# A hybrid encoder block: gate and up projections of ten pairs as token-major quads, activations turned by VectorE and moved within SBUF

## The chip, the cores and the metric

The kernel runs on one core of a Trainium2 chip. The metric is the device time of one execution in microseconds; the time before is the median of three runs. A profile is one execution recorded by the hardware profiler. Its engines are TensorE (PE, with its weight loads as PEld), VectorE (DVE), ScalarE (ACT), GpSimd (POOL) and SyncE (SP), which issues DMA transfers; ACT and POOL issue some too.

## The reference

One layer of an encoder block on 512 tokens of width 1024, in float32: a combined input projection feeds a short convolution and a bidirectional retention, the two are gated and merged, and a feed-forward part follows. The change is in the feed-forward part:

```
h2 = rmsnorm(x, g_ffn)
x  = x + (silu(h2 @ w_ff_gate) * (h2 @ w_ff_up)) @ w_ff_down     # 1024 -> 2816 -> 1024
y  = rmsnorm(x, g_final)
```

## The kernel before

**Precision and Strassen.** Every matrix operand is split into a high and a low part (`split`, L200: ACT rounds to the high part at L203, VectorE subtracts to get the low part at L204), and each product is three matmuls: high by high, high by low, low by high. On top of that the large products use a Strassen scheme in Winograd's form: seven products of half-size operands in place of eight. The operand forms are called a11, a12, a22, s1 to s4 for activations and b11, b21, t1 to t4, b22 for weights. Weight forms t1 to t4 are sums of two weight quarters; VectorE adds them (L301) right before the split, except for a few weights listed in `SUMMED`, whose sums are made ahead of time in DRAM by accumulating transfers and only loaded.

**Two ways to lay out a product.** Feature-major (`prod`, L375, matmuls at L383): weights are the stationary operand, activations are the moving one, 256 columns per matmul, the result has features on the partitions and tokens along the free dimension. Token-major (`prod_tm`, L409, matmuls at L427): activations are stationary, weights are the moving operand, 512 columns per matmul, the result has tokens on the partitions. The mixers' projections, the output projections and the down product are token-major already.

**The feed-forward part before.** The 2816 inner features are 22 blocks of 128, or 11 pairs. A pair (`pair`, L1173) is one Strassen product whose two weight columns are 256 gate features and the same 256 up features; its seven products are feature-major, 24 narrow matmuls each. The results come out with features on the partitions, which is what the down product needs for its stationary operand, so `gated` (L1125) can build the activation forms at once: silu on ACT, a multiplication by the up half on VectorE (L1139), differences (L1155) and splits into high and low tiles. The first products of up to three pairs are run ahead (`FIRST_PRODUCTS`, `beside`). The pairs are worked in three parts of 3, 4 and 4 (`FF_PARTS`), each followed by its down product (`strassen` through `down`, L1223), in which two pairs' worth of rows are one unit of 512 columns by two. The first part's result is put in DRAM (`put_first`), added to the residual `ydr` later (`add_first`, behind a small POOL instruction called mark), the second part's is accumulated into `ydr` directly (`add_y`); the last part's joins the residual in SBUF (`snap_y`, `to_y`), is normalized and written out (`put`).

**What sets the order.** `plan` lists all weight units in the order of use. `take` (L321) hands out the next unit and splits ahead until `AHEAD` = 2 units are ready; `load_raws` keeps the raw loads on SP `LEAD` = 4 units ahead of that. The tile framework schedules instructions at compile time; each engine then works its own queue in order, with semaphore waits. `tc.issue_after` orders an engine's instructions behind a given one. Pools are small: 14 large tiles (`big`), of which the gate/up input's forms hold seven and one part's activation forms seven, 9 tiles of 512 columns (`tmp`), 8 PSUM banks, 2 tiles in `misc`.

## Time and profile before

| | before |
|---|---|
| median of three runs | 1023.7 us |
| lowest of them | 1023.23 us |
| span of the profiled execution | 1021.7 us |
| the runs' median less that span | 2.0 us |
| TensorE busy | 1013.2 us, 5586 matmuls |
| VectorE busy | 902.5 us |
| ScalarE busy | 548.4 us |
| GpSimd busy | 151.7 us |
| mean granted TensorE clock | 0.999 |
| read from HBM, written | 162.82 MB, 57.41 MB |

The profiled execution's own time is not given apart from its span; the last instruction ends 1021.7 us after the first, and the runs' median is 2.0 us above that. Busy time counts an engine's instructions, not its waits. Matmuls are pipelined, so their price is read from the distance of starts or from a stretch of the chain divided by its count, not from the duration of one. "Idle before" in a group of instructions is the time the engine stood still ahead of them, with what ended it. The feed-forward part runs from about 689 us to the end.

### The profile page before, as it was taken

The numbers are of one execution on the slowest core, as the hardware profiler recorded it, in microseconds if no ns is written. First come the engines' busy times: TensorE is split into PE (matmuls) and PEld (weight loads), VectorE is DVE, ScalarE is ACT, GpSimd is POOL, SyncE is SP. The second block draws the span as 40 slices with busy tenths as digits, with TensorE's granted clock in tenths as the row PEclk, the third lists the DMA queues.
The fourth block names the chain that finished last, engine by engine and source line by source line (L and its number), as shares of the span: only waits on it lengthen the run. The fifth ranks groups of instructions, "written<-read, shape, count | busy, mean of one in ns | idle before, by whom it ended". The sixth has DMA issues, their size and how long they took to land.

```text
span 1021.7 us, 14821 instructions
## 1 busy us (share of the span) xinstructions
PE 1013.2 (99%) x5586; PEld 883.2 (86%) x5586; DVE 902.5 (88%) x1161; ACT 548.4 (54%) x744; POOL 151.7 (15%) x238
## 2 busy tenths in 40 slices
PE   9999999999999999999999999999999999999997
PEld 7888888888888998888888888889998999899986
DVE  7878998979798888797989997999898999889996
ACT  7547665553655455343543325586654565556554
POOL 0030221222122003202122100020001410110011
PEclk9999999999999999999999999999999999999999
DMA  9525587695767657839597855484316562663523
GB/s 354 188 81 185 173 296 212 214 310 162 249 196 238 250 203 268 333 130 349 124 331 294 272 200 169 157 264 132 107 42 242 172 154 83 198 153 104 165 69 98
DMA packets 53992, 202.34 MB, mean 198 GB/s; under 512 B 7392, under 2 KB 7520, under 8 KB 49312
## 3 DMA queue, kind: packets, MB, share of 16 engines
q1 hardware_dynamic: 37600, 137.39, 39.0%
q0 software_dynamic: 16032, 63.71, 21.3%
q8 instruction: 44, 0.72, 0.3%
q10 hardware_dynamic: 288, 0.29, 0.1%
q14 instruction: 28, 0.23, 0.1%
HBM read 162.82 MB, written 57.41 MB: 216 GB/s over the span
## 4 chain that ended last, share of the span: by engine, by line
PE 98%; DVE 1%; ACT 0%; issue 0%; POOL 0%; POOLq 0%; ACTq 0%
PE bank L427 39%; PE bank L383 27%; PE bank L342 10%; PE bank L343 10%; PE bank L344 10%; PE bank L477 0%; PE bank L1053 0%; PE bank L998 0%; PE bank L662 0%; DVE raw L301 0%; DVE big L1296 0%; ACT whi L203 0%; DVE wlo L204 0%; POOL fin L1286 0%; POOL ac L1035 0%
## 5 line engine op out<-in xcount | busy, mean ns | idle before, releaser
L203 ACT CAST whi<-raw 128x1024 fp32r<-128x1024 f32 (+2 forms) x299 | 302.8, 1028 | 265.0 <-PE bank L427 67.1
L204 DVE TENSOR_TENSOR wlo<-raw,whi 128x1024 fp32r<-128x1024 f32 (+2 forms) x300 | 352.7, 1192 | 68.0 <-ACT whi L203 67.7
L383 PE MATMUL bank<-xform,whi 128*128 128x256 f32 x1424 | 258.2, 284 | 0.3 <-ACT whi L203 0.3
L383 PEld LDWEIGHTS bank<-xform,whi 128*128 128x128 f32 x1424 | 222.3, 192 | 2.0 <-ACT t L434 0.8
L383 PE MATMUL bank<-xform,wlo 128*128 128x256 f32 x712 | 200.7, 283 | 0.0
L427 PE MATMUL bank<-whi,big 128*128 128x512 f32 x596 | 187.0, 389 | 0.0
L427 PE MATMUL bank<-whi,xform 128*128 128x512 f32 x496 | 157.1, 390 | 0.0
L301 DVE TENSOR_TENSOR raw<-raw 128x1024 f32<-128x1024 f32 (+1 forms) x128 | 152.0, 1203 | 4.2 <-DMA raw<-wquad 3.3
L383 PEld LDWEIGHTS bank<-xform,wlo 128*128 128x128 f32 x712 | 136.4, 192 | 0.0
L427 PEld LDWEIGHTS bank<-whi,big 128*128 128x128 f32 x596 | 111.9, 188 | 23.8 <-ACT t L434 0.4
L427 PE MATMUL bank<-wlo,big 128*128 128x512 f32 x298 | 115.7, 389 | 0.0
L427 PEld LDWEIGHTS bank<-whi,xform 128*128 128x128 f32 x496 | 93.0, 188 | 19.7 <-DVE xform L204 0.6
L427 PE MATMUL bank<-wlo,xform 128*128 128x512 f32 x248 | 96.5, 389 | 0.0
L434 ACT COPY t<-bank 128x512 f32<-128x512 f32 x105 | 61.0, 587 | 56.3 <-PE bank L383 30.1
L342 PE MATMUL bank<-big,whi 128*128 128x512 f32 x220 | 85.7, 390 | 0.0
L344 PE MATMUL bank<-big,wlo 128*128 128x512 f32 x220 | 85.6, 389 | 0.0
L343 PE MATMUL bank<-big,whi 128*128 128x512 f32 x220 | 85.6, 389 | 0.0
L427 PEld LDWEIGHTS bank<-wlo,big 128*128 128x128 f32 x298 | 56.0, 188 | 11.4
L427 PEld LDWEIGHTS bank<-wlo,xform 128*128 128x128 f32 x248 | 46.6, 188 | 9.6
L342 PE MATMUL bank<-whi,big 128*128 128x512 f32 x128 | 49.8, 389 | 0.0
L343 PE MATMUL bank<-wlo,big 128*128 128x512 f32 x128 | 49.8, 389 | 0.0
L344 PE MATMUL bank<-whi,big 128*128 128x512 f32 x128 | 49.8, 389 | 0.0
(203 smaller groups left out, 1385.8 us busy)
## 6 DMA issues: line engine op xcount, KB each, us to landing
raw<-wquad SPq DMA_DIRECT2D x140, 512.0 KB, 4.7
raw<-wpack SPq DMA_DIRECT2D x42, 512.0 KB, 6.3
t_f<-wquad POOLq DMA_DIRECT2D x12, 512.0 KB, 8.0
z<-t POOLq DMA_DIRECT2D x24, 256.0 KB, 4.5
t_o<-wquad POOLq DMA_DIRECT2D x12, 512.0 KB, 6.7
zform<-z POOLq DMA_DIRECT2D x6, 1024.0 KB, 7.8
v<-t POOLq DMA_DIRECT2D x16, 256.0 KB, 5.7
sg<-t POOLq DMA_DIRECT2D x16, 256.0 KB, 4.8
```

The source lines that it names most:

```text
L203: first = (round or nc.scalar.copy)(hi, src)
L204: low_of[0] = nc.vector.tensor_tensor(out=lo, in0=src, in1=hi.bitcast(F32), op=ALU.subtract)
L301: nc.vector.tensor_tensor(out=t, in0=t, in1=raws[quad, more, u][:, 0:n], op=ALU.add)
L342: nc.tensor.matmul(ps, lh, rh, start=first, stop=False)
L343: nc.tensor.matmul(ps, lh, rl, start=False, stop=False)
L344: nc.tensor.matmul(ps, ll, rh, start=False, stop=last)
L383: nc.tensor.matmul(o, l[:, c], r[:, k], start=start and s == 0 and k == 0 and i == 0, stop=stop and k == 3 and i == 2, skip_group_check=True)
L427: nc.tensor.matmul(pss[tt], l, r[:, c], start=start and k == 0 and i == 0, stop=stop and k == n - 1 and i == 2, skip_group_check=True)
L434: nc.scalar.copy(t, ps)
```

## The change

Ten of the eleven pairs are joined two by two into five quads, the eleventh (`LONE`) stays a feature-major pair. A quad is a token-major Strassen product with 512 gate columns and 512 up columns: `first_a`, `first_b` and `rest` run the seven products through `prod_tm`, in two weight units of four blocks' rows each. `SUMMED` names one quad instead of two pairs, which is the same amount of weights. The parts are now 4, 4 and 3 pairs.

A quad's results have tokens on the partitions. `gated` forms silu times up on a 128x512 tile as before, and then VectorE transposes its 32x32 blocks into two tiles called turned (two transposes of 128x256 per tile, eight per quad). That leaves 32-row blocks at the wrong partitions; `scatter` moves them with 16 SBUF-to-SBUF transfers of 32 rows by 512 columns (64 KB), issued by POOL, into the space where the low parts of two forms will lie. `forms_of`, called after the fifth product of the following quad (in the lone pair after its fourth), builds the activation forms from there: one split of 1024 columns, one of 512, four differences and four splits of 512; it is ordered behind the last weight split issued.

The transposes leave tokens in an order in which each block of 128 holds four runs of 32 rows. So the rows of the residual and of the output are addressed by `rows` as 4 runs of 32 rows for each block: the accumulating writes to `ydr`, the loads of it at the end and the writes of the output all use it.

The order of the work: products of quads 0 and 1, quad 2, the down product of quads 0 and 1, quads 3 and 4, the down product of quads 2 and 3, the lone pair, the last down product of quad 4 and the lone pair.

```diff
-FF_PARTS = ((0, 3), (3, 4), (7, 4))
+FF_PARTS = ((0, 4), (4, 4), (8, 3))
+LONE = NFB // 2 - 1
...
-SUMMED = (("f", 0), ("f", 1), ("o",))
+SUMMED = (("g", 0), ("o",))
...
+    f(0, "b11", "b21")
+    f(1, "b11")
+    f(0, "t2", "t1", "t3", "t4", "b22")
+    f(1, "t1", "t2", "b21", "t3", "t4", "b22")
+    f(2, *FORMS)
+    d(*FF_PARTS[0])
+    f(3, *FORMS)
+    f(4, *FORMS)
+    d(*FF_PARTS[1])
+    f(LONE, *FORMS)
+    d(*FF_PARTS[2])
...
+    def act_forms_of(q, n, x1, x2):
+
+        tiles, i = slot(q)
+        hi, lo = ({k: area(t[j], i, n, k) for k, t in tiles.items()} for j in range(2))
+        split(flat(x1), flat(hi["a"]), flat(lo["a"]))
+        split(pairs(x2, 1), pairs(hi["z"], 0), pairs(lo["z"], 0))
+        x = [pairs(t, e) for t in (x1, x2) for e in range(2)]
+        s1, s3, s2, s4 = (t512()[:, 0:256 * n].rearrange("p (b t) -> p b t", t=P) for _ in range(4))
+        for o, a, b, op in ((s1, x[2], x[3], ALU.subtract), (s3, x[0], x[2], ALU.subtract),
+                            (s2, s1, x[0], ALU.subtract), (s4, x[1], s2, ALU.add)):
+            nc.vector.tensor_tensor(out=o, in0=a, in1=b, op=op)
+        for k, e, t in (("v", 1, s1), ("v", 0, s3), ("w", 0, s2), ("w", 1, s4)):
+            split(t, pairs(hi[k], e), pairs(lo[k], e))
...
+    def gated(i, j, g, u):
+
         s = t512()
         gate_of[0] = s
         nc.scalar.activation(s, g, AF.Silu)
         nc.vector.tensor_tensor(out=s, in0=u, in1=s, op=ALU.mult)
...
+        if i not in turned:
+            turned[i] = [misctile(D, "turned").rearrange("p (q i j r) -> p q i j r", q=2, i=4, j=4) for _ in range(2)]
+        for h, t in enumerate(turned[i]):
+            nc.vector.transpose(t[:, :, :, j, :].rearrange("p q i r -> p i q r"),
+                                s.rearrange("p (i q c) -> p i q c", i=4, q=4)[:, :, 2 * h:2 * h + 2, :])
+
+    def scatter(i):
+
+        tiles, at = slot(2 * i)
+        x = [area(tiles[k][1], at, 2, k).bitcast(F32) for k in "wv"]
+        for b in range(NB):
+            o = x[b // 2][:, b % 2].rearrange("p q e t -> p (q e t)")
+            for q in range(4):
+                nc.gpsimd.dma_start(o[32 * q:32 * q + 32],
+                                    turned[i][q // 2][32 * b:32 * b + 32, q % 2].rearrange("c i j r -> c (i j r)"))
+        scattered[i] = x
+
+    def forms_of(i):
+        with tc.issue_after(hi_of[0].ins), tc.issue_after(low_of[0].ins):
+            act_forms_of(2 * i, 2, *scattered[i])
...
+    def first_a(i, *between):
+
+        a = [bank(), bank()]
+        for u, hook in zip((0, 2), between or (None, None)):
+            prod_tm(4, of(XF[0, 0]), a, True, part=(u,))
+            if hook:
+                hook()
+        heads_of[i] = a, [snap(x) for x in a]
...
+    def rest(i, last_first=False, middle=True, behind=None):
+
+        a, p1 = heads_of[i]
+        d = [bank(), bank()]
+        if not last_first:
+            prod_tm(4, of(XF["s1"]), d, True)
+        prod_tm(4, of(XF["s2"]), a, False)
+        u2 = [snap(x) for x in a]
...
+        prod_tm(4, of(XF["s3"]), a, False)
+        u3 = [snap(x) for x in a]
+        for tt in range(2):
+            nc.vector.tensor_tensor(out=u3[tt], in0=d[tt], in1=u3[tt], op=ALU.subtract)
         if behind:
+            behind()
+        prod_tm(4, of(XF[1, 1]), a, False, True)
+        for tt in range(2):
+            gated(i, 2 + tt, a[tt], u3[tt])
+        prod_tm(4, of(XF["s4"]), d, False, True)
+        for tt in range(2):
+            nc.vector.tensor_tensor(out=u2[tt], in0=d[tt], in1=u2[tt], op=ALU.subtract)
+            gated(i, tt, p1[tt], u2[tt])
...
+    yrows = ydr.rearrange("(j b r) d -> b j r d", j=4, b=4)
+
+    def rows(nb, half, of=yrows):
+        return of[nb][:, :, half * 512:(half + 1) * 512]
 
     def add_y(t, nb, half):
-        nc.gpsimd.dma_start(out=ydr[nb * P:(nb + 1) * P, half * 512:(half + 1) * 512], in_=t, accum_op=ALU.add)
+        nc.gpsimd.dma_start(out=rows(nb, half), in_=t, accum_op=ALU.add)
...
+    rest(0, last_first=True, middle=False)
+    scatter(0)
+    rest(1, behind=lambda: forms_of(0))
+    scatter(1)
+    quad(2, lambda: forms_of(1))
+    down(4, put_first)
+    scatter(2)
+    quad(3, lambda: forms_of(2))
+    mark = small.tile([P, 1], F32, tag="mark", name="mark", bufs=1)
+    add_first(nc.gpsimd.tensor_scalar_add(mark, gate_of[0][:, 0:1], 0.0))
+    scatter(3)
+    quad(4, lambda: forms_of(3))
+    down(4, add_y)
+    scatter(4)
+    lone(lambda: forms_of(4))
...
     for half in (1, 0):
-        nc.sync.dma_start(y[half][:, 2:4, :], ydr[2 * P:, half * 512:(half + 1) * 512].rearrange("(n p) c -> p n c", p=P))
+        for nb in (2, 3):
+            nc.sync.dma_start(y[half][:, nb, :], rows(nb, half))
...
         for t, j, q in ((last, half, nc.sync), (other, 1 - half, nc.scalar if nb == 1 else nc.sync)):
-            q.dma_start(out[nb * P:(nb + 1) * P, j * 512:(j + 1) * 512], t)
+            q.dma_start(rows(nb, j, outrows), t)
...
+    outrows = out.rearrange("(j b r) d -> b j r d", j=4, b=4)
...
+        elif kind == "g":
+            w = (gate, up)[c].reshape(2, 4, P, -1)[r, u:u + n // 512, :, q[0] * 512:q[0] * 512 + 512]
```

More of the change, by code (lines that the diff above doesn't have):

```diff
@@ L115, in f, with d @@
         for n in names:
[L116 to L129 removed]
+            if q == LONE:
+                out.append(("q", ("f", q), n, 0, 4))
+            else:
+                for u in (0, 2):
+                    out.append(("q", ("g", q), n, u, 2))
+    def d(q0, n):
         units = [(name, u) for name in FORMS for u in range(0, n, 2)]
@@ L209, in split @@
                 op0=ALU.mult, op1=ALU.subtract)
+        hi_of[0] = first
         return first
@@ L1113, in block_kernel @@
     act = {}
[L1114 to L1135 removed]
+    slots = {}
@@ new lines, in lone_gated @@
+    def lone_gated(th, g, u):
+        s = t512()
+        nc.scalar.activation(s, g, AF.Silu)
+        if not lone_x:
+            lone_x.extend(t512().rearrange("p (b q e t) -> p b q e t", b=2, q=1, e=2) for _ in range(2))
+        for b, o in enumerate(lone_x):
+            for e in range(2):
+                x, y = (t.rearrange("p (e j b r) -> p e b j r", e=2, j=2, b=4)[:, e, 2 * b:2 * b + 2] for t in (u, s))
+                z = o[:, :, 0, e, 64 * th:64 * th + 64].rearrange("p b (j r) -> p b j r", j=2)
+                nc.vector.tensor_tensor(out=z, in0=x, in1=y, op=ALU.mult)
@@ L1136, in gated, with lone, ev11 @@
+    lone_x = []
+    def lone(behind):
+        got = {}
+        def ev11(t):
+            got.update(g=t)
+            behind()
+        forms = {"a11": XF[0, 0], "a12": XF[1, 0], "a22": XF[1, 1], **{n: XF[n] for n in ("s1", "s2", "s3", "s4")}}
+        fm_quad(forms, ev11, lambda ps: lone_gated(1, ps, got["u"]),
+                lambda t: got.update(u=t), lambda t: lone_gated(0, got["g"], t))
+        act_forms_of(LONE, 1, *lone_x)
+    turned = {}
+    def gated(i, j, g, u):
         s = t512()
@@ L1139, in gated @@
         nc.vector.tensor_tensor(out=s, in0=u, in1=s, op=ALU.mult)
-        def both(j, t):
-            split(t.rearrange("p (s t) -> p s t", s=2), *(x[:, :, i, :] for x in gates[q0][j]))
-        E, O = slice(0, 256), slice(256, 512)
-        if th == 1:
-            split(s[:, O], *(x[:, i, :] for x in act["a22"]))
-        else:
-            both(0, s)
-        gates[q, th] = s
-        if (q, 1 - th) not in gates:
-            return
-        x1, x2 = gates.pop((q, 0)), gates.pop((q, 1))
-        v, w = t512(), t512()
```

149 lines of the change are left out of this document (48 added, 101 removed).

## The prediction

> **What bounds the kernel now.** I read the page first: how much of the span each engine works, and which engine the chain of waits runs through.
>
> ```profile
> span 1021.7 us, 14821 instructions
> PE 1013.2 (99%) x5586; PEld 883.2 (86%) x5586; DVE 902.5 (88%) x1161; ACT 548.4 (54%) x744; POOL 151.7 (15%) x238
> PE 98%; DVE 1%; ACT 0%; issue 0%; POOL 0%; POOLq 0%; ACTq 0%
> ```
>
> TensorE is the bound: it is never without work for long, and 98% of the chain is its own instructions. So only cheaper matmuls can shorten the kernel, and VectorE, at 88%, is the engine that can spoil it. The profiled execution's span is 1021.7 us; the runs' median of 1023.7 us is 2.0 us more, which I take as what lies around the span. The sum below is made on 1021.7 and the 2.0 is added back.
>
> Second, the chain in order of time (start, duration, what) gives the price of a matmul in either form. L383 is the feature-major product of a gate/up pair (256 columns each), L427 the token-major product (512 columns); 73 to 226 us is a stage of token-major quads with the same code the change will use.
>
> ```profile
> 73.07 152.49 PE bank L427 x672
> 787.53 73.91 PE bank L383 x612
> 861.44 38.11 PE bank L427 x168
> 899.55 71.99 PE bank L383 x600
> ```
>
> The 512-column matmul takes 152.49/672 = 0.2269 us, the 256-column one 73.91/612 = 0.1208 or 71.99/600 = 0.1200 us. Two narrow ones cost 0.2408 us where one wide one costs 0.2269: about 13 ns per instruction goes on top of the columns.
>
> Third, busy time by stage (length, then PE, weight load, DVE, ACT and POOL, with counts): pair 2, pairs 3 to 6, the second down product, most of pairs 7 to 10.
>
> ```profile
> 728.00:757.00 29.00, 28.96 (x241) 28.89 (x241) 28.52 (x39) 16.67 (x26) 0.00 (x0) 1.00 0.27 83
> 787.50:861.40 73.90, 73.87 (x613) 73.71 (x614) 69.63 (x85) 44.79 (x60) 14.96 (x11) 1.00 0.55 150
> 861.40:899.50 38.10, 38.10 (x171) 31.54 (x169) 34.86 (x39) 20.16 (x25) 5.26 (x6) 1.00 0.57 149
> 899.50:971.50 72.00, 72.00 (x602) 72.00 (x601) 65.68 (x81) 40.24 (x53) 1.73 (x2) 1.00 0.48 142
> ```
>
> TensorE has no gap in any of them and its granted clock is 1.00. VectorE stands at 94% in the pairs (69.63/73.90), and for 29 us at 98% (28.52/29.00) without TensorE losing anything; that is the margin the change draws on. ACT has 40% to spare.
>
> **The matmuls.** Ten of eleven pairs become five quads. A pair is 7 products of 24 narrow matmuls; ten pairs are 1680. A quad is 7 products of 24 wide ones; five are 840. 1680 x 0.1204 (mean of the two rows) = 202.3 us against 840 x 0.2269 = 190.6: a saving of 11.7 us (11.0 to 12.3 by the one narrow row or the other). The eleventh pair stays narrow, and the down products keep their 462 wide matmuls, regrouped 4, 4, 3. All of it is on the path.
>
> The Trainium skill, "TensorE: Matmul & The Clock Gate", section "Wait — 56ns, not 53.3ns?", speaks against this gain: back-to-back matmuls take N/2.4 GHz and 2.5 ns. By that rule 1680 of 109.2 ns are 183.4 us and 840 of 215.8 ns are 181.3, an estimate of 2.2 us saved. The trace disagrees (120 and 227 ns), and the measurement decides.
>
> **VectorE, per quad.** The starts in this stretch of its timeline give the pitch of an instruction, which is shorter than its duration, since the next one starts before the end.
>
> ```profile
> 802.15 0.69 DVE L1139 TENSOR_TENSOR t<-t,t 128x512 f32<-128x512 f32 x1
> 802.75 1.22 DVE L301 TENSOR_TENSOR raw<-raw 128x1024 f32<-128x1024 f32 x1
> 803.89 0.42 DVE L204 TENSOR_TENSOR big<-t,big 128x256 fp32r<-128x256 f32 x1
> 804.23 0.69 DVE L1200 TENSOR_TENSOR t<-bank,t 128x512 f32<-128x512 f32 x1
> 443.03 11.44 DVE L218 STREAM_TRANSPOSE big<-big 32x512 f32<-32x512 f32 x16
> ```
>
> So 512 elements per partition take 0.60 us, 1024 take 1.14, 256 take 0.34, and a transpose of 512 takes 11.44/16 = 0.715. Two pairs today: 14 weight splits and 8 weight sums, 22 x 1.14 = 25.1; 6 evictions, 3.6; 4 gate multiplications, 2.4; activation forms, 6 splits of 512, 2 of 256, and 8 differences of 256, 7.0. Sum 38.1 us beside 336 x 0.1204 = 40.5 of TensorE: 94%, as the stage shows.
>
> A quad after: the same 25.1, 3.6 and 2.4. The forms come in larger pieces (one split of 1024, one of 512, four differences and four splits of 512): 6.5. New are 8 transposes of 128x256. The trace has only 32x512; if partitions are free, as a 128x512 operation that costs 0.60 suggests beside 0.715 for 32x512, the price goes by elements: 0.715 minus 256 at 1.0 ns (0.60 less 0.34 over 256) = 0.455 us, 3.6 a quad. From below 0.34 (a plain operation), 2.7; from above 1.43 (twice as many 32x32 blocks as the row's, each at the row's price), 11.4. I take 3.6. Sum 41.2 us beside 168 x 0.2269 = 38.1 of TensorE: VectorE is 3.1 us over in each of quads 1 to 4. Quad 0 loads its weight sums ready made, so 9.1 less, and it has the forms of its input to make, as before. The lone pair, with the forms of quad 4 in it, asks 11 x 1.14 + 3 x 0.60 + 8 short multiplications (0.2 each, the 0.34 less 128 elements) + 6.5 = 22.4 beside 168 x 0.1204 = 20.2.
>
> What hides the excess are the two down products: 22 x 1.14 + 6 x 0.60 = 28.7 of 38.1 us each. Splits for what follows can run ahead there by two or three units (2.3 to 3.4 us), and the last quad's gates and transposes (6 us) can slip into it. Of 6.2 us over in quads 1 and 2, and again in 3 and 4, I leave 1.5 each on the path, 0.5 for the lone pair: **+3.5 us**, between 0 and the full 4 x 3.1 + 2.2 = 14.6.
>
> **The moves.** Each quad's transposed gates go through 16 POOL transfers of 64 KB, 80 in all; their forms, one quad later, wait for them on ACT and VectorE, and behind those waits stand weight splits. TensorE holds two split units then, 2 x 12 x 0.2269 = 5.4 us. POOL's own rows around today's second and third stage:
>
> ```profile
> 773.64 1.20 POOL L1211 DMA_DIRECT2D first_part<-t  x2 [85.15 <-DVE t L448]
> 805.94 7.34 POOL L1247 TENSOR_SCALAR mark<-t 128x1 f32<-128x1 f32 x1 [17.56 <-DVE t L1139]
> 813.24 6.82 POOL L1208 DMA_DIRECT2D ydr<-first_part  x8
> 900.32 1.73 POOL L1208 DMA_DIRECT2D ydr<-t  x2 [3.83 <-DVE t L464]
> big<-ydr POOLq DMA_DIRECT2D x4, 256.0 KB, 4.5
> ```
>
> At 0.6 us an issue, 16 take 9.6 us and land 4.5 later: 14 us. For quads 0, 1 and 2 the forms come behind five products of the next quad, 5 x 24 x 0.2269 = 27.2 us later, or the down product lies between: hidden. Quad 3's stand behind the mark (7.3) and the eight additions (6.8): with some 4 us to the last gate, 4 + 7.3 + 6.8 + 14.1 = 32.2 against 27.2, five late. Quad 4's stand behind the down product's last additions, whose issue ends 2.5 us past the down (902.05 less 899.5): 2.5 + 14.1 = 16.6, against four narrow products, 4 x 24 x 0.1204 = 11.6; five late again. The units in hand and splits put ahead of the forms cover most: I take **+2.5 us** for both, from 0 to 10. Their 1 MB per quad is small beside stages whose engines are half idle (0.48 to 0.57 above).
>
> **The end.** The last product has 18 wide matmuls instead of 24: 4.1 us from the second last's eviction to the end, where the chain has 1014.44 - 1010.21 = 4.2 us of other work:
>
> ```profile
> 1010.21 0.69 DVE big L1273
> ...
> 1013.89 0.55 POOL fin L1286
> ```
>
> +0.2. The output is written with the same eight transfers of 256 KB, their rows now in four runs of 32. Sum: 1021.7 - 11.7 + 3.5 + 2.5 + 0.2 = 1016.2, with the 2.0 around it **1018.2 us**; with each term at its likely ends 1011 to 1027.
>
> **Rivals.** *A quarter of the DMA engines at the end* (slower). Output and residual blocks become 4 runs x 32 rows x 512 columns. No transfer of before has an outer count of four, so the trace shows neither its cost nor its absence; the nearest rows are today's output writes, which use all 16 engines (the first row lists 40 slices of 1010 to 1022 us, the second issues and time to landing):
>
> ```profile
> GB/s 0 0 0 0 0 0 0 0 335 362 335 396 314 7 0 362 369 389 375 253 259 375 382 382 341 7 0 0 0 239 375 396 375 348 14 0 0 0 0 0
> y<-big SPq DMA_DIRECT2D x7, 256.0 KB, 2.1
> 1011.59 6.71 SPq L1300 DMA_DIRECT2D y<-big  x7
> ```
>
> If such a pattern is dealt to four engines, it moves at 396/4 = 99 GB/s: 2.65 us for each write, 21.2 for eight that start at 1012.4 (slice 8): they end at 1033.6 instead of 1020.3 (slice 34), +13.3. It decides as soon as a write takes longer than the 0.84 us from one issue to the next (6.71 over eight). Time 1018.2 + 13.3 = 1031.5, 1024 to 1040 with the terms above; the four residual loads, 10.6 us of the same engines, delay the weight loads queued behind them on SP, which two or three units loaded ahead cover. The Trainium skill, "DMA: Bandwidth & Descriptors", section "Why a DMA increments its semaphore by 16 and not by 1", says so: a transfer uses the largest number of engines up to 16 that divides the outermost size of both patterns, here four. No run here shows it yet.
>
> *VectorE becomes the bound* (slower). The queue is in order, so nothing may slip into the downs: all 14.6 us appear in place of 3.5, 1018.2 + 11.1 = 1029.3, 1023 to 1036; with transposes by blocks still more. For it: 94% already, and in-order waits. Against: TensorE has no wait today at that level.
>
> *The gain in full*, every cover holding: 1023.7 - 11.7 = 1012.0; this is the low end of the forecast rather than a case apart.
>
> **Chances.** The forecast 0.45, quarter of the engines 0.33, VectorE 0.17, elsewhere 0.05. The range 1011 to 1035 leaves out a tail of the two rivals and little below. 2%, about what a measurement here tells from no change, is 20.5 us: faster than 1003.2 exceeds the whole saving, 0.01; slower than 1044.2 needs both rivals at once, 0.05; within, 0.94.
>
> **What would show it.** Today's last matmul:
>
> ```profile
> 1015.23 0.39 PE L427 MATMUL bank<-whi,big 128*128 128x512 f32 x1
> ```
>
> From its end at 1015.6 the span runs on for 6.1 us. The same after the change would refute the first rival, some 19 would confirm it. Further: 1680 matmuls fewer at the narrow line and 840 more at the wide one, those of gate/up at 0.227 us in the chain; transposes near 0.45 us; VectorE at 97% or more in quads 1 to 4; TensorE waiting there some 6 us in all for weight splits that stand behind forms, and these for moved blocks. The prediction is wrong if wide matmuls cost more in gate/up, or if TensorE's waits exceed 12 us.

## The result

The changed kernel takes 1155.5 us (1154.6 to 1156.2) where the kernel before takes 1023.4: a ratio of 1.1284 on record, with a 95% interval of 1.1267 to 1.1301. Four runs of the kernel before are on record, three of 1023.2 to 1023.7 us and a disturbed one of 1690.6, which the ratio leaves out and which the median of 1023.7 ahead of the prediction still had among its three. The forecast was 1018.2, and the range ended at 1035.

The page of the changed kernel first: span, busy time by engine, the rate of the DMA in 40 equal slices, and the chain that ended last by engine.

```profile
span 1154.5 us, 13314 instructions
PE 1016.1 (88%) x4746; PEld 845.1 (73%) x4746; DVE 913.8 (79%) x1179; ACT 548.7 (48%) x736; POOL 189.5 (16%) x318
GB/s 329 165 64 264 247 210 213 311 157 238 231 243 186 284 318 153 291 202 252 301 245 184 151 251 172 131 99 146 162 183 67 171 67 46 122 37 154 48 24 73
PE 71%; issue 14%; DVE 6%; DMA 3%; POOL 3%; ACT 1%; POOLq 0%; DVEq 0%; ACTq 0%
```

The 840 matmuls fewer are there (5586 to 4746). TensorE's share of the chain has fallen from 98% to 71%, and 14% is "issue": an engine stood before an instruction of its own queue with nothing that the profile shows to wait for. The last ten slices move some 81 GB/s on average, the thirty before them 213. The windows by stage say where it begins (length, then PE, weight load, DVE, ACT and POOL with counts, granted clock, DMA share, GB/s):

```profile
689.00:732.00 43.00, 43.00 (x194) 35.46 (x193) 42.69 (x50) 30.15 (x38) 0.00 (x0) 1.00 0.43 136
772.00:811.00 39.00, 37.83 (x166) 30.63 (x164) 38.96 (x50) 23.28 (x30) 2.65 (x6) 1.00 0.37 121
887.00:925.00 38.00, 36.33 (x159) 29.41 (x158) 35.70 (x35) 18.98 (x22) 3.32 (x3) 1.00 0.50 139
925.00:963.00 38.00, 6.22 (x25) 4.17 (x24) 7.96 (x7) 4.13 (x4) 8.55 (x13) 0.66 0.33 68
1001.00:1045.00 44.00, 14.36 (x109) 13.69 (x107) 9.41 (x9) 6.49 (x7) 9.82 (x15) 0.70 0.32 45
1130.00:1154.50 24.50, 0.00 (x0) 0.00 (x0) 1.56 (x3) 1.44 (x3) 0.55 (x1) 0.53 0.23 84
```

Up to 925 us TensorE loses little (1.2 of 39 us and 1.7 of 38 in the rows shown). Then it works 6.22 of 38 us, and 14.36 of 44; no engine is busy for even a third of these stretches, so something that isn't an engine's work sets the time. At the very end there are 24.5 us without a matmul, where there were 6.1. POOL's timeline (start, duration, operation, idle before it and what ended that) shows what sets it:

```profile
884.17 0.22 POOL L1306 TENSOR_SCALAR mark<-t 128x1 f32<-128x1 f32 x1 [38.05 <-DVE t L1193]
884.59 1.20 POOL L1271 DMA_DIRECT2D ydr<-first_part  x1 [0.20 <-issue]
893.41 1.11 POOL L1271 DMA_DIRECT2D ydr<-first_part  x1 [7.62 <-issue]
902.22 1.10 POOL L1271 DMA_DIRECT2D ydr<-first_part  x1 [7.70 <-issue]
...
953.42 1.11 POOL L1271 DMA_DIRECT2D ydr<-first_part  x1 [7.62 <-issue]
954.08 3.96 POOL L1207 DMA_DIRECT2D big<-turned  x7
962.35 4.65 POOL L1207 DMA_DIRECT2D big<-turned  x9 [4.31 <-DMA ydr<-first_part]
```

The eight additions to the residual, 6.82 us of issuing in the kernel before, are 8.5 to 15 us apart here and hold POOL's queue for 70 us. Quad 3's moved blocks stand behind them and go out at 954 us where they would have gone at about 891. Rows of the waits from 690 us to the end (total, times, longest) carry that on: POOL at its own issues, ACT for the moved blocks, TensorE for ACT; and, in the last down product, VectorE for the residual's loads and TensorE for VectorE. Four of those loads are POOL's, which adds them as they land; they stand 9.6 to 9.8 us apart from 1081.69 us on.

```profile
POOL ydr L1271 <- issue: 107.4, 14, 14.2
ACT big L200 <- DMA big<-turned: 68.3, 4, 37.7
PE bank L381 <- ACT t L432: 35.8, 2, 35.6
PE bank L425 <- ACT big L200: 33.6, 2, 32.1
DVE bank L1383 <- DMA big<-ydr: 22.2, 2, 13.3
PE bank L425 <- DVE bank L1383: 19.9, 2, 11.1
PE bank L425 <- DVE wlo L201: 16.0, 6, 9.2
```

And the end: the last matmul in the timeline, then the DMA's share of all engines in tenths and its rate, in 40 slices of 1125 to 1154.5 us.

```profile
1128.90 0.39 PE L425 MATMUL bank<-whi,big 128*128 128x512 f32 x1
```

```profile
DMA  0000022222222222222222222222222222221000
GB/s 0 0 0 0 8 25 14 56 78 97 103 103 103 103 100 100 94 69 83 94 97 103 83 83 72 97 103 103 100 100 106 103 103 100 103 78 53 28 0 0
```

The output's writes run at 2 tenths of the engines and at up to 103 GB/s, where those of the kernel before ran at up to 396. That is the first rival's pattern: 256 KB at 103 GB/s are 2.5 us a write (2.65 were forecast). The Trainium skill, "DMA: Bandwidth & Descriptors", section "Why a DMA increments its semaphore by 16 and not by 1", gives the rule of it, four engines for an outermost size of four; the trace agrees.

### The profile page after: what moved, and what is told of

Same layout as the page of the kernel before. It is cut to its first block, busy times and chain, and to the rows that moved or that the text cites. A ratio compares the mean times of both kernels' runs of the same rounds, so it can differ in the third digit from the quotient of the medians.

```text
span 1154.5 us, 13314 instructions
## 1 busy us (share of the span) xinstructions
PE 1016.1 (88%) x4746; PEld 845.1 (73%) x4746; DVE 913.8 (79%) x1179; ACT 548.7 (48%) x736; POOL 189.5 (16%) x318
## 4 chain that ended last, share of the span: by engine, by line
PE 71%; issue 14%; DVE 6%; DMA 3%; POOL 3%; ACT 1%; POOLq 0%; DVEq 0%; ACTq 0%
PE bank L425 38%; PE bank L340 9%; PE bank L341 9%; PE bank L342 9%; PE bank L381 5%; DMA big<-turned 2%; DVE wlo L201 1%; POOL ydr L1271 1%; POOL big L1207 1%; DVE raw L299 1%; DMA big<-ydr 1%; DVE big L201 1%; DMA ydr<-first_part 1%; DVE t L1157 1%; ACT whi L200 1%
## 5 line engine op out<-in xcount | busy, mean ns | idle before, releaser
L425 PE MATMUL bank<-whi,xform 128*128 128x512 f32 x1056 | 331.0, 390 | 1.1 <-ACT whi L200 1.1
L425 PE MATMUL bank<-whi,big 128*128 128x512 f32 x596 | 195.0, 402 | 58.2 <-ACT big L200 33.6
L425 PEld LDWEIGHTS bank<-whi,xform 128*128 128x128 f32 x1056 | 197.7, 188 | 44.0 <-ACT whi L200 2.0
L425 PE MATMUL bank<-wlo,xform 128*128 128x512 f32 x528 | 205.8, 390 | 3.0 <-DVE wlo L201 3.0
L425 PEld LDWEIGHTS bank<-wlo,xform 128*128 128x128 f32 x528 | 99.1, 188 | 24.2 <-DVE wlo L201 3.8
L381 PE MATMUL bank<-xform,whi 128*128 128x256 f32 x304 | 57.6, 291 | 35.8 <-ACT t L432 35.8
L201 DVE TENSOR_TENSOR big<-big 128x1024 fp32r<-128x1024 f32 (+1 forms) x22 | 23.7, 1098 | 69.9 <-ACT big L200 69.9
L381 PEld LDWEIGHTS bank<-xform,whi 128*128 128x128 f32 x304 | 49.3, 199 | 36.6 <-ACT t L432 36.5
L1207 POOL DMA_DIRECT2D big<-turned x80 | 41.5, 609 | 93.3 <-issue 46.8
L200 ACT CAST big<-big 128x1024 fp32r<-128x1024 f32 (+1 forms) x22 | 20.8, 950 | 69.2 <-DMA big<-turned 68.3
L340 PE MATMUL bank<-whi,big 128*128 128x512 f32 x128 | 49.8, 389 | 0.0
## 6 DMA issues: line engine op xcount, KB each, us to landing
zform<-z POOLq DMA_DIRECT2D x6, 1024.0 KB, 7.6
```

What stands on the lines that cost most here:

```text
L200: first = (round or nc.scalar.copy)(hi, src)
L201: low_of[0] = nc.vector.tensor_tensor(out=lo, in0=src, in1=hi.bitcast(F32), op=ALU.subtract)
L340: nc.tensor.matmul(ps, lh, rh, start=first, stop=False)
L381: nc.tensor.matmul(o, l[:, c], r[:, k], start=start and s == 0 and k == 0 and i == 0, stop=stop and k == 3 and i == 2, skip_group_check=True)
L425: nc.tensor.matmul(pss[tt], l, r[:, c], start=start and k == 0 and i == 0, stop=stop and k == n - 1 and i == 2, skip_group_check=True)
L1207: nc.gpsimd.dma_start(o[32 * q:32 * q + 32], turned[i][q // 2][32 * b:32 * b + 32, q % 2].rearrange("c i j r -> c (i j r)"))
```

## The experiments

e5, e7, e11, e12, e14 to e16 and e18 compute the whole layer. In the others rows of the residual or of the output don't meet the right tokens, so they leave out the order of the tokens (e6 has the runs without the transposes that call for them); where one copies in place of transposing, it leaves out the turning too. e2 to e6 are one execution each. Each ratio is to the kernel before as it ran beside that kernel, 1023.2 to 1024.0 us.

### Which use of the four runs costs what (e1 to e4)

e1 gives residual and output 128 consecutive rows; e2 keeps the four runs for the output alone, e3 for the residual alone, e4 has 16 runs of 8 rows for both.

```diff
-    yrows = ydr.rearrange("(j b r) d -> b j r d", j=4, b=4)
+    yrows = ydr.rearrange("(n p) d -> n p d", n=4)
-    outrows = out.rearrange("(j b r) d -> b j r d", j=4, b=4)
+    outrows = out.rearrange("(n p) d -> n p d", n=4)
```

> The changed kernel with one thing undone: residual and output blocks are again 128 consecutive rows, in place of 4 runs of 32. (It leaves out the putting back of the token order, so the rows of the output and of the residual do not meet the right tokens.) Theory A, the pattern of 4 runs is the whole loss: the accumulating writes to the residual issue on POOL within 2 us of each other again instead of every 8.5 us, quad 3's moved blocks are there in time, TensorE has no wait over 5 us, the run ends some 6 us after the last matmul, and the time is the 1018 us of the prediction's own sum (1011 to 1027). Theory B, the pattern is only a part and the 80 moves of blocks through POOL or VectorE's load cost by themselves: 1030 to 1100 us, with TensorE still waiting for moved blocks.

> As e1, but the eight output writes keep their 4 runs of 32 rows (the residual is plain, so the rows of the residual do not meet the right tokens). Theory A, a write of 4 runs uses a quarter of the DMA engines: from the last matmul to the end of the span 25 us as in the changed kernel (1129.3 to 1154.5) instead of 6; the whole is 19 us above e1. If the long tail of the changed kernel came from what was late before it (residual loads on the same engines), the tail is under 12 us here.

> The complement of e2: the accumulating writes to the residual and its loads keep the 4 runs, the output is written in blocks of 128 consecutive rows (output rows in turned order). Theory A: POOL's accumulating transfers stand 8.5 us apart, TensorE loses some 105 us between 925 and 1130 us as in the changed kernel, and the tail after the last matmul is 6 us: 1155 - 19 = 1136 us. Theory that the output's writes matter for more than the tail: under 1120 us.

> The changed kernel with its row pattern cut finer: a block is 16 runs of 8 rows in place of 4 runs of 32 (so rows of residual and output do not meet the right tokens), same three dimensions, same 2 KB per row. Theory A, what counts is that the outermost size is 4 and so a quarter of the engines is used: with 16 the transfers go back to all engines, POOL's accumulating writes stand under 2 us apart, and the time is that of e1 within 5 us. Rival C, any pattern of separated runs is slow (more addresses for POOL to write out, scattered rows in DRAM): as slow as the changed kernel, about 1155 us, or slower.

Measured: e1 1030.6 us, ratio 1.0079 (1.0055 to 1.0104); e2 1050.8; e3 1134.3; e4 1038.3. Over e1, the output's pattern costs 20.2 and the residual's 103.7; together 123.9 of the 124.9 that separate e1 from the whole change. (That it adds up to within 1 us is in part luck: e1's own four runs take 1028.0 to 1034.7.) So the pattern of the rows makes all but the 7.0 us that e1 stands above the kernel before, five sixths of it by the residual. With 16 runs POOL's eight additions take 6.97 us again and 11.0 us follow the last matmul in place of 25.2: it is the number of outer runs, not their being in pieces. (e4's 7.7 us over e1 lie outside its theory's 5, in 925 to 963 us, where TensorE works 29.82 of 38 at a granted clock of 0.91: it waits 2.1 us for a form of quad 3, which stands at 936 us on ACT in place of 904, and 3.3 us for an eviction behind the forms. Why the form stands later no run shows.)

### What holds POOL (e5)

An addition to four runs could be slow for POOL to issue, or POOL could be waiting for room in which to put its descriptors. e5 is the whole change with four times that room (and two raw buffers fewer, to make place).

```diff
-dynamic_dma_scratch_size=2048
+dynamic_dma_scratch_size=8192
```

> The changed kernel with four times the space for the descriptors that POOL writes (8192 in place of 2048), paid for with 8 raw weight tiles in place of 10. Why does POOL stand 8.5 us between two accumulating transfers of 4 runs? Theory D, the descriptors of one such transfer, on a quarter of the engines, fill their rings, and the next transfer waits until they are worked off: with four times the space several issue in a row, the first three of the eight additions of the first part within 5 us instead of 18, and quad 3's moved blocks come earlier, total under 1120 us. Theory E, POOL waits for the transfer itself for another reason (the additions are ordered one after another): spacing stays 8.5 us and the total is 1155 us or a little more for the missing raw tiles.

Measured: 1064.9 us instead of 1155.5. POOL's timeline:

```profile
885.02 7.96 POOL L1271 DMA_DIRECT2D ydr<-first_part  x7 [0.96 <-issue]
```

Seven additions go out back to back in 7.96 us. So issuing was never slow, and room is what was missing: with 2048 bytes an addition was issued some 8.5 us after the one before, which is the median time to landing of one addition in that trace. The 34 us that stay over e1 are the end (25.5 us after the last matmul) and the blocks, which still wait for the additions' DMA as late as 910 us.

### The pattern alone in the kernel before (e6)

```diff
-    nc.gpsimd.dma_start(out=ydr[nb * P:(nb + 1) * P, half * 512:(half + 1) * 512], in_=t, accum_op=ALU.add)
+    nc.gpsimd.dma_start(out=rows(nb, half), in_=t, accum_op=ALU.add)
```

> The kernel before with the row pattern alone: additions to the residual, its loads at the end and the output writes in 4 runs of 32 rows per block (its rows then do not meet the right tokens). No blocks are moved, so nothing waits on POOL except the additions themselves. Theory A: the tail grows by 19 us, the four accumulating loads of the last part stand 8.5 us apart and make TensorE wait some 15 to 20 us in the last down product, and before that no loss: 1023.6 + 19 + 17 = 1060 us (1045 to 1075). That the 4-run pattern costs the changed kernel 130 us is then the moved blocks queued behind it. If the pattern itself were the loss: 1130 us or more here too.

Measured: 1110.1 us, 86.9 more than without the pattern and with nothing else of the change; the expectation was 50 too low. So two thirds of the 131.9 us lost come without a moved block. In POOL's timeline the additions stand just as far apart,

```profile
813.67 1.20 POOL L1213 DMA_DIRECT2D ydr<-first_part  x1
822.17 1.11 POOL L1213 DMA_DIRECT2D ydr<-first_part  x1 [7.30 <-issue]
```

and the tiles of the down product stay taken until POOL has added them. ACT's next evictions wait for that, one after the other; the last of them (ACT's timeline):

```profile
979.18 0.58 ACT L434 COPY t<-bank 128x512 f32<-128x512 f32 x1 [17.58 <-DMA ydr<-t]
```

TensorE waits 42.7 us for this one. The expectation had little standing behind the additions where no blocks do; what stands behind them are buffers.

### What is left with plain rows: VectorE (e8), POOL's order (e9), both (e10)

e1 is 7.0 us above the kernel before, where the forecast was 5.5 below it: its theory A missed by 3 us, and it lies at the low end of theory B. Its timelines show two things: short waits of TensorE at the ends of four quads, and one of 3.53 us at 914 for an eviction. On ACT that eviction is queued behind a form of quad 3, which waits for the moved blocks:

```profile
911.34 0.62 ACT L200 CAST big<-big 128x512 fp32r<-128x512 f32 x1 [6.41 <-DMA big<-turned]
911.86 1.99 ACT L200 CAST whi<-raw 128x1024 fp32r<-128x1024 f32 x2
913.75 1.07 ACT L432 COPY t<-bank 128x512 f32<-128x512 f32 x2
```

e8 is e1 with the transposes as copies on ACT; e9 is e1 with `scatter(3)` in front of the mark, by which the blocks go out ahead of all but two of the additions; e10 has both.

```diff
-            nc.vector.transpose(t[:, :, :, j, :].rearrange("p q i r -> p i q r"),
+            nc.scalar.copy(t[:, :, :, j, :].rearrange("p q i r -> p i q r"),
...
+    scatter(3)
     mark = small.tile([P, 1], F32, tag="mark", name="mark", bufs=1)
     add_first(nc.gpsimd.tensor_scalar_add(mark, gate_of[0][:, 0:1], 0.0))
-    scatter(3)
```

> The run with plain rows, and VectorE's 40 transposes replaced by plain copies of the same size on ScalarE (it leaves out the turning of the blocks). It takes 40 x 0.41 = 16 us from VectorE, 3.3 us a quad. Theory F, VectorE's excess over TensorE in quads 1 to 4 causes the waits of about 2 us for a weight split at the end of each quad there: these waits vanish, and the time falls by 6 to 9 us from the plain run, to 1019 to 1024. Theory G, the waits come from the order of the queues and not from VectorE's load: they stay, and the time is within 3 us of the plain run.

> The run with plain rows, and quad 3's moved blocks put on POOL's queue ahead of six of the eight additions of the first part (in place of behind all eight), so they are asked for some 5 us earlier and do not stand behind 2 MB of additions. Theory H: in the plain run TensorE's wait of 3.5 us at 914 us, with weights late before it and a clock step down after it, comes from those blocks being late: it goes, and the time falls by 4 to 7 us, to 1023 to 1027. If the blocks are not late because of the additions: within 2 us of 1030.

> Both: the 40 transposes as plain copies on ScalarE (the turning of the blocks is left out) and quad 3's blocks ahead of most additions. In the run with the first alone the waits at the ends of quads 1 to 4 were gone, but one wait of 18.4 us for quad 3's blocks took their place (POOL's mark had taken 6.9 us there in place of 0.2). Theories F and H together: both kinds of wait go, and the time is that of the matmuls saved: 1013 to 1019 us, faster than before. If the queue order was not the cause of the 18.4 us: 1030 or more.

Measured: e8 1034.7, ratio 1.0113 (1.0096 to 1.0130); e9 1025.2, 1.0010 (1.0000 to 1.0019); e10 1027.3, 1.0035 (1.0021 to 1.0048). e9 takes the wait at 914 away. What remains in it are the quads' ends; TensorE's timeline at two of them:

```profile
769.55 0.73 PE L425 MATMUL bank<-whi,xform 128*128 128x512 f32 x2 [0.82 <-ACT whi L200]
771.88 0.68 PE L425 MATMUL bank<-wlo,xform 128*128 128x512 f32 x1 [1.59 <-DVE wlo L201]
...
773.22 0.63 PE L425 MATMUL bank<-wlo,xform 128*128 128x512 f32 x1
773.64 0.63 PE L425 MATMUL bank<-whi,xform 128*128 128x512 f32 x1
...
811.73 0.73 PE L425 MATMUL bank<-whi,big 128*128 128x512 f32 x2 [0.32 <-ACT whi L200]
813.88 0.50 PE L425 MATMUL bank<-wlo,big 128*128 128x512 f32 x1 [1.41 <-DVE wlo L201]
```

At the first, 3.1 us are lost around two waits (2.4 of them as idle time in the rows), and then the matmuls start 0.42 us apart (773.22 to 773.64) instead of 0.227 until 775.6, another 1.5; the granted clock is 0.53 from 772 to 775.6 us and 1.00 before and behind. At 811 and the two later ends it is 2.2 to 2.3 us each, and the clock stays at 1.00. Together 11.4 us. The Trainium skill, "TensorE: Matmul & The Clock Gate", section "Part 1: The HAM clock gate (the "warmup" mystery)", has the array at half rate after an idle window of some 3.4 us, which it calls free-running. The half rate agrees with the 0.42 us. The window isn't shown: no idle time here is longer than 1.6 us, and in e1, e12 and the changed kernel two waits as long (0.72 and 1.60 us in e1) leave the clock at 1.00. So the 1.5 us are chance on top of the waits.

e8 and e10 missed their expectations, but for a reason that has nothing to do with the matmuls. The chain of e10 runs from the start of the feed-forward part through three quads, a down product and half of the next quad without a wait, and so does e8's (171.62 us):

```profile
692.13 171.55 PE bank L425 x756
```

Then comes POOL's mark, 0.22 us in the changed kernel:

```profile
881.39 15.89 POOL L1307 TENSOR_SCALAR mark<-t 128x1 f32<-128x1 f32 x1 [40.13 <-DVE t L1193]
```

It takes 15.89 us (15.88 in e8, not the 6.9 of e10's expectation), everything of POOL's goes out late, and TensorE waits 11.2 us (18.4 in e8) for an eviction that stands behind the blocks' forms on ACT.

### Without the mark (e13)

e10 with the mark removed and all additions behind `scatter(3)`:

```diff
-    mark = small.tile([P, 1], F32, tag="mark", name="mark", bufs=1)
-    add_first(nc.gpsimd.tensor_scalar_add(mark, gate_of[0][:, 0:1], 0.0))
+    add_first(moved[0])
```

> The run with plain rows, transposes as plain copies on ScalarE (the turning is left out) and quad 3's sixteen moves ahead of all eight additions, without POOL's mark: the additions stand behind the last of those moves instead. In the last run with both changes the mark, an operation on one column, had held POOL for 15.9 us, and quad 3's blocks behind it made TensorE wait 11.2 us. Theories F and H: without it no wait over 2 us is left in quads 1 to 4, TensorE ends at about 1005 us, and the time is 1023.9 - 11.7 + 3 of tail = 1015 us (1012 to 1018), faster than before. If 1022 or more, what holds the change back is neither VectorE's share nor the queue of POOL.

Measured: 1012.8 us (1012.7 to 1012.8), ratio 0.9893 (0.9877 to 0.9910). Its chain:

```profile
690.84 261.29 PE bank L425 x1152
952.13 14.41 PE bank L381 x120
```

1152 wide matmuls, all but 24 of those of quads 0 to 4 and two down products, in 0.2268 us each and without one wait; the lone pair's narrow ones at 0.1201. So the gain on which the forecast stood is real, though only in a kernel that leaves the turning out. What ate it in e9 are the transposes on VectorE: e8 and e10 have the mark and no waits at the quads' ends, e14 below has no mark and all of them. The last matmul stands at 1001.5 us here and at 1014.5 in e9, 13 us, of which 11.4 are the quads' ends and 1.5 a later start of the part.

### Whole kernels (e7, e11, e12, e14 to e16)

Can the whole computation have this? In e7 the residual is written once in the turned order, by transfers of 32 rows, and so is the output: consecutive rows, no four runs. e11 adds e9's order and shares the output's strips among SP, ACT and POOL; e12 also has quad 1's weight sums made ahead in DRAM; e14 is e11 without the mark and with no strips on POOL; e15 splits three units ahead instead of two; e16 adds the sums.

```diff
-            q.dma_start(rows(nb, j, outrows), t)
+            for i in range(4):
+                o = i * P + nb * 32
+                q.dma_start(out[o:o + 32, j * 512:(j + 1) * 512], t[32 * i:32 * i + 32])
```

> The changed kernel with the token order put right without the 4-run pattern: the residual is written once, ahead of the feed-forward part, in the turned order, by transfers of 32 rows (32 of 64 KB in place of 8 of 256 KB), so that additions and loads are plain; the output is written in 32 transfers of 32 rows. Nothing is left out. Theory A: the time of the run with plain rows, 1028 to 1031 us, plus 1 to 4 us at the end for four times as many issues: 1029 to 1035. If small transfers are themselves dear (80 more moves than before were not, in the plain run), over 1040.

> A whole kernel, nothing left out: residual written once in turned order and output written in transfers of 32 rows, quad 3's blocks ahead of most additions, and the 32 output transfers dealt to SP, POOL and ACT in place of 28 on SP (in the run before, SP's 28 issues at 0.42 us each took 15 us of the tail). Expected: the plain run with blocks first plus 2 to 4 us of tail: 1025 to 1031, against 1040 with SP alone.

> As e11, and quad 1's weight sums t1 to t4 too are made ahead in DRAM, by 16 more POOL transfers during the retention stage; VectorE is spared 8 sums of 1.14 us in quad 1, 9 us. Theory F: the waits at the end of quads 1 and 2 go, 4 to 6 us less than e11: 1020 to 1026. If the additional DRAM traffic in the retention stage holds its loads up, as slow as e11 or slower.

> A whole kernel: residual in turned order, output in strips of 32 rows on SP and, for the last block, SP and ACT in turn, quad 3's moves ahead of all additions and no mark. VectorE keeps its transposes, so the waits of some 2 us at the end of quads 1 to 4 stay. Expected: TensorE ends as in e11 (1014.4) or 1 us earlier, the tail is 11 us instead of 13.9: 1025 to 1028.

> As e14, with three weight units split ahead of use in place of two. The waits at the end of quads 1 to 4 are for weight splits that stand on VectorE's queue behind the gates, transposes and forms of one quad's end; if it is the bunching of that work and not VectorE's sum over the stage, one unit more (2.7 us of TensorE) covers it: the waits go, 1017 to 1021 us. If VectorE's sum is what counts (101 to 108% of TensorE in those quads), the waits are only put off: 1024 to 1028.

> As e15, and quad 1's weight sums made ahead in DRAM, which spares VectorE 9 us in quad 1. By the sum over the stage this takes 3 to 5 us more off; by the bunching alone it takes nothing more from e15. Expected 1016 to 1022.

Measured: e7 1040.3, ratio 1.0166 (1.0151 to 1.0182); e11 1029.8, 1.0055 (1.0040 to 1.0070); e12 1029.3, 1.0063 (1.0043 to 1.0082); e14 1034.6, 1.0107 (1.0092 to 1.0122); e15 1036.6, 1.0126 (1.0111 to 1.0142); e16 1038.1, 1.0143 (1.0128 to 1.0158). None beats the kernel before, and only e11 is as fast as expected. All of them are far under the 1155.5 of the change, and two things keep them from e13's time.

The strips: 28 of them on SP take 15.26 us to go out in e7 and e14, 2.3 of it a wait for an earlier strip's DMA, and the end after the last matmul is 18 us (13.9 in e11, 9.0 with plain rows).

The quads' ends: e14 has no mark and has them all the same. VectorE's timeline at the first of them:

```profile
762.98 1.27 DVE L1260 TENSOR_TENSOR t<-bank,t 128x512 f32<-128x512 f32 x2
764.17 1.27 DVE L1195 TENSOR_TENSOR t<-t,t 128x512 f32<-128x512 f32 x2
765.37 1.41 DVE L1199 STREAM_TRANSPOSE turned<-t 128x256 f32<-128x256 f32 x4
766.72 3.44 DVE L299 TENSOR_TENSOR raw<-raw 128x1024 f32<-128x1024 f32 x3
770.08 2.35 DVE L201 TENSOR_TENSOR wlo<-raw,whi 128x1024 fp32r<-128x1024 f32 x2
```

From 762.98 to 770.08 it splits nothing: evictions, gates, transposes, three weight sums. TensorE has two units, 5.4 us. In the window of the first such end VectorE is busy for 39.09 us in e14,

```profile
732.00:772.00 40.00, 37.72 (x165) 30.61 (x164) 39.09 (x52) 20.18 (x27) 12.95 (x27) 0.99 0.48 145
```

and with the sums made ahead, in e12, 33.95. TensorE loses as much, so it isn't the amount in quad 1 alone:

```profile
732.00:772.00 40.00, 37.61 (x164) 30.33 (x163) 33.95 (x48) 20.66 (x27) 12.76 (x26) 1.00 0.53 155
```

The third unit shortens the waits for splits in this part (4.9 us in e15 against 7.4 in e14), but the part begins 2.5 us later and the last matmul stands 3.3 us later, at 1017.3 instead of 1014.0: the expectations of e15 and e16, 16 to 22 us lower, failed; e14 itself is 7 us above its own, by the 18 us at the end where 11 were expected.

### The place of the gates in the queue (e17, e18)

e17 is e9 without the mark, and with the last two gates and four transposes of each quad behind the splits of three units of what follows. e18 is the same with the whole computation, its strips shared by SP, ACT and POOL.

```diff
+        def gates():
+            with tc.issue_after(low_of[0].ins):
+                for tt in range(2):
+                    gated(i, tt, p1[tt], u2[tt])
+            scatter(i)
+        waiting.append([3, gates])
```

> Plain rows, the blocks of every quad moved ahead of the additions, no mark (leaves the order of tokens out as the plain rows do), transposes kept on VectorE; the last product's two gates and four transposes of each quad stand behind the splits of three units of what follows, in place of ahead of them. If the waits at the quads' ends (about 2.5 us and some lost clock at each of four) come from where the bunch of gates, transposes and sums stands in VectorE's queue, most of them go: last matmul at 1004 to 1010 us, time 1015 to 1021 us. If VectorE simply has more work than a quad lasts (41 us against 38), they come back at a later unit: last matmul at 1012 to 1016, time 1022 to 1026.

> The whole computation: the same order of the gates, residual and output in strips of 32 rows, the output's strips shared by SP (16), ACT (8) and POOL (8, behind its last small operation). By the first theory the last matmul is at 1004 to 1010 us, and the strips end 11 to 12 us after it instead of 18: 1018 to 1024 us. By the second 1025 to 1030.

Measured: e17 1023.2, ratio 0.9996 (0.9987 to 1.0005); e18 1028.3, 1.0051 (1.0037 to 1.0064). e17's time lies in the second theory's range. Its last matmul starts at 1010.5, between the two theories and 4 us ahead of e9's (1.3 of it an earlier start of the part). Its waits, none of them long any more:

```profile
PE bank L425 <- DVE wlo L201: 4.2, 7, 1.1
PE bank L425 <- ACT t L438: 1.5, 1, 1.5
```

Moved, the bunch makes smaller waits elsewhere, 5.7 us in place of e9's 7.6. So the place in the queue is part of the cause and VectorE's work another; how much is which stays open. Only taking the transposes off VectorE (e13) took all of it, and no run has the turning itself on another engine. e18 ends 14 us after its last matmul, 4 us less than with 28 strips on SP and no better than e11, where 11 to 12 were expected: SP issues a strip every 0.46 us or so, but stands 4.2 us for an earlier one's DMA.

## Why the prediction was wrong

The sum was wrong by 137 us, and one step of it makes nearly all: **the residual's additions**. The prediction took POOL's price for them from the row of the kernel before (813.24, 6.82 us for eight, where the change needs 70) and looked at the pattern of four runs only where transfers are read and written at the end, "the four residual loads, 10.6 us of the same engines" (SP's; the four that POOL adds were not priced either). It asked what four engines make of a write's time, and not what they make of the room for descriptors on POOL's queue. The first rival had the mechanism and put it in the wrong place: at the end it costs 20.2 us (e2), in the middle 103.7 (e3), because 16 additions and then four accumulating loads are held there one behind the other. Behind the additions stand quad 3's and quad 4's blocks, and the tiles of the down products stay taken meanwhile, for which TensorE waits 42.7 us at once in e6, where no blocks are moved. The prediction did name those blocks as standing behind the eight additions; only the additions' price was that of the kernel before.

The other steps:

**The matmuls**, -11.7: right. 0.2268 us a wide and 0.1201 a narrow one (e13). e13's last matmul gains 13.7 us: of the other 2.0, 1.1 lie ahead of the part, which starts at 686.4 in place of 687.5 us, and 0.9 in it. They aren't waits, of which the two kernels have 2.1 and 2.2 us. That e13's 1012.8 us are so near the third rival's 1012.0 is luck: these 2.0 and the 2.9 of the end, below, nearly cancel.

**VectorE**, +3.5 between 0 and 14.6: too low, 11.4 (e9), inside the bounds. The transposes were cheaper than taken, not dearer: 0.34 us from one start to the next (four in the 1.35 us from 765.37 to 766.72 in e14) against 0.455. What failed is "what hides the excess are the two down products": the queue is in order, and the bunch at a quad's end comes before any down product. By the measured price a quad asks 40.3 us of VectorE beside 38.1 of TensorE, an excess of 2.2 us, which is just what three of the four ends lose, so the sum of a quad would give the same number. Against the sum alone stand e12, which takes work from quad 1 and leaves the wait at its end, and e17; how much is which stays open. The prediction's second rival had the queue in order; that its time, 1029.3, is close to e1's 1030.6 is in part luck, since it gave the whole cost to VectorE.

**The moves**, +2.5 for quads 3 and 4: 5.4 between e1 and e9 by their times, 2.3 by their profiled spans. The mark, priced at 7.3 us, took 0.22, and the blocks were late all the same (6.41 us on ACT in e1), by the additions ahead of them: with the blocks first the wait is gone.

**The end**, +0.2: 9.0 us after the last matmul in e1, e9 and e13 against 6.1, so +2.9. The step counted the last product's length against one chain of work behind the product before it. But the last splits and the tiles before it stand on VectorE ahead of that product's last eviction, which comes 1.6 us before the last matmul's end in e1 (5.4 in the kernel before), so nearly all of four tiles' normalizations are left for afterwards.

**What would show it**: "some 19 would confirm" the first rival at the end; it was 25.2. The writes began 1.9 us later against the last matmul than forecast (at about 1128.0, its end at 1129.3) and ran for some 25 us in place of 21.2, at 103 GB/s only part of the time. The prediction's limit, TensorE's waits over 12 us, was passed ninefold (111 us), and first at the place that it gave for the moved blocks. (Its 0.84 us from one issue to the next divides 6.71 us by eight, where the row has seven; 0.96 leads to the same.)

## What to carry to other kernels

When a change alters an access pattern, price every transfer that uses it, and for each of GpSimd's ask two things: on how many engines it lands, and what stands behind it if the next one can't be issued before it has landed. Work added to an engine that is nearly full is weighed by where it bunches in that engine's in-order queue as well as by its sum over a stage: here eight transposes of 0.34 us in each quad, 10.9 us before four quads' ends, cost 11.4 us, where the room in the down products was to hide most of it. And where a change as a whole is far off, run the pattern, the order and the engine's share each by itself: the gain was there (0.9893 in e13).

## What the runs showed of the hardware

- A 256 KB accumulating transfer to 4 runs of 32 rows held GpSimd's queue for 8.5 to 15 us with 2048 bytes of descriptor space (changed kernel, e3, e6) and 1.1 us with 8192 (e5, seven in 7.96 us); to 16 runs of 8 rows (e4) or 128 consecutive rows (e1) it took some 0.87 us with 2048.
- The mark, GpSimd's addition on one column, took 0.22 us in the changed kernel, e1 and e9, 7.34 in the kernel before, 15.88 in e8 and 15.89 in e10. In e8 VectorE works through operations on two tiles in SBUF from the mark's start at 880.13 on without a gap, and the mark ends at 896.01, in VectorE's first gap (its timeline below); e10 is the same. In the kernel before there is no gap: the mark, begun at 805.94, ends at 813.28, just after VectorE has begun, at 813.20, an operation with one of its two tiles in PSUM; in e6 these are 813.72 and 813.62. In e1 transposes, of one tile, run beside it. The Trainium skill, "GPSIMD Engine Reference", section "1. Specifications", has GpSimd share its SBUF interfaces with VectorE and lists contention with VectorE's instructions of two SBUF inputs. All of these runs fit that; none varies VectorE's inputs alone.

```profile
893.56 2.37 DVE L201 TENSOR_TENSOR wlo<-raw,whi 128x1024 fp32r<-128x1024 f32 x2
896.19 1.23 DVE L201 TENSOR_TENSOR wlo<-raw,whi 128x1024 fp32r<-128x1024 f32 x1 [0.26 <-ACT whi L200]
```

- After the two waits at the first quad's end (0.82 and 1.59 us in e9) TensorE's granted clock was 0.53 for 3.6 us in e9, and matmuls started 0.42 us apart; e2, e4, e7, e11 and e14 have the slow stretch too. After waits as long in e1 (0.72 and 1.60 us), e12 and the changed kernel the clock stayed at 1.00. So the length of the waits doesn't decide it; what does, no run shows.
